# A two-layer gated trunk on one core: Silu in one ScalarE function, another order in the first output pair, the last merged chunk turned a slot later

## The chip, the cores and the metric

The kernel runs on one core of one Trainium2 chip. The metric is the device time of one execution in microseconds (us). All tensors are float32.

## What is computed

The reference is a trunk of two layers over a sequence of 256 positions with a model width of 2048:

```
for l in range(2):
    h = rms_norm(x, mix_norm[l])
    q, k, v, uv, gate_logits = split(h @ w_in[l])
    branch_a = sliding_window_attention(rope(rms_norm(q)), rope(rms_norm(k)), v, sinks[l]) @ w_attn_branch[l]
    branch_b = chunked_sgu(gelu(uv), ...) @ w_sgu_branch[l]
    gates = sigmoid(gate_logits)
    merged = gates[:, :2048] * branch_a + gates[:, 2048:] * branch_b
    x = x + merged @ w_out[l]
    h2 = rms_norm(x, ffn_norm[l])
    x = x + (silu(h2 @ w_gate[l]) * (h2 @ w_up[l])) @ w_down[l]
```

The hidden width of the last line is 5632, that is 11 chunks of 512 columns. The change touches the product with `w_out`, the norm behind it and the `silu` line.

## The kernel before, in words

**Entries.** Every product with a weight is cut into *entries*: 256 rows of a weight by a chunk of 512 columns. An entry is one DMA of 512 KB into a tile `raw` (line 202, on SyncE's queue), one ScalarE copy that rounds it to `whi` (L228), one VectorE subtraction that gives the rest `wlo` (L229), and the matmuls at L324 and L325. These take three terms: `whi` times the high part `uh` of the activations, `wlo` times `uh`, `whi` times the low part `ul`. A common entry has 12 matmuls of 128 x 512. Two chunks of columns that share their activations go as a *pair*: the first four 256 x 512 blocks of a pair are done by a seven-product scheme (entries P1 to P7, six matmuls each; some need a VectorE subtraction of weights at L213, and results are kept and moved at L346 to L352), and the rest by common entries, G for the first chunk and U for the second (lines 129 to 149). For the seven products, chunk 0 of the activations is needed whole (`uh`, `ul`) and as four sums of its quarters (`sh`, `sl`).

**Order.** The list `entries` (lines 172 to 186) fixes TensorE's order. The head of a pair (P1, P5, P2, P6, P7, P4) is woven into the last entries of the plan ahead of it. `Stream.next` (L233) loads seven entries ahead and splits four ahead. `whi` and `wlo` have four buffers each, so the split of an entry can only start when TensorE is done with the entry four before it. TensorE's instructions stand as they are written; for the other engines a scheduler sets the order of what is written.

**Slots.** All other work is put into slots by `after(n, fn)`: `fn` is written n slots later, and a slot is one common entry or two of six matmuls (lines 246 to 255, 359 to 363).

**Turning.** Activations are turned (transposed) for use as the stationary side, in `transposed` (L404). Mostly VectorE transposes blocks of 32 x 32 into a tile `box` (L393), and sixteen DMAs of 32 KB gather them into `tt` (L399), all on GpSimd's queue or, with `queue=None`, every second one on SyncE's. With `on_pe`, TensorE turns them into `pt` by eight small matmuls (L436). Then ScalarE makes `uh` (L418, L422, or `flat` at L463 and `uh` at L467 for chunk 0), and VectorE makes `ul` (L419, L427, L468). There is one `box`.

**Around the change.** The four chunks of `merged` are made by the four products `sgu` (line 944): VectorE adds the branches per half of the positions at L947 and L949 into the tile `gate`. Chunk 3, the last, is turned on TensorE (`on_pe`) three slots after its sums. The pair of chunks 0 and 1 of `w_out` follows ("first output pair"), then the pair of chunks 2 and 3 ("second output pair"), then the FFN's pairs of `w_gate` and `w_up`. When a chunk of the output is done, `residual` (L867) adds it into `xs` at L875, turns it two slots later for the FFN (`nxt.unit`), and squares it for the norm (L505). Chunk 0 goes through the steps of `WINO_NORM`, six numbers of slots counted from the turn: two scalings, the split, two groups of sums, the split of the sums. The norm's factor r (`rstd`) is applied only when products leave PSUM.

**The FFN's gate.** With g the gate product before r, `on_gate` (L965 to L968) takes th = tanh(r g / 2) on ScalarE (L967, scale `rhalf`), and (th + 1) g on VectorE (L968); `on_up` multiplies by the up product and by r r / 2 (`rr`, L972). It runs for 11 chunks in each of two layers, with two halves of the positions each.

Of the kernel before, what the change touches and what calls it, by code (L numbers as in the profile page):

```python
# [10 lines left out]
AF = mybir.ActivationFunctionType  # L11
# [17 lines left out]
NCH = D // CW  # L29
# [2 lines left out]
W_LOAD = 7  # L32
ROUNDS = ((0, 4), (4, 8), (8, 11))
WINO = 0
WINO_NORM = 7, 8, 10, 11, 12, 13
WINO_IN = 6, 7, 8, 12, 13, 14
WINO_FIRST = 6, 7, 8, 9, 10, 11
WINO_MIX = 6, 7, 9, 10, 11, 13
# [19 lines left out]
def hybrid_trunk(ctx: ExitStack, tc: tile.TileContext, x, mix_norm, w_in, q_norm, k_norm, sinks,  # L58
# [28 lines left out]
    def tiny(n, name, bufs=None):  # L87
        return small.tile([P, n], F32, tag=f"{name}{n}", name=nm(name), bufs=bufs)
# [32 lines left out]

        return Plan(key, [], [half(w, h, "X") for h in range(w.shape[0] // (2 * P))])

    def pair(key, wa, wb, by_unit=False):

        h1, h2 = 2 * WINO, 2 * WINO + 1
        l11, l12, l21, l22 = (load_of(w, h, t) for w, h, t in ((wa, h1, "k11"), (wb, h1, "k12"), (wa, h2, "k21"),  # L130
                                                              (wb, h2, "k22")))
        k11, k12, k21, k22 = l11[0], l12[0], l21[0], l22[0]
        rest = [h for h in range(wa.shape[0] // (2 * P)) if h // 2 != WINO]
        g, u = [half(wa, h, "G") for h in rest], [half(wb, h, "U") for h in rest]
        head = [dict(tag="P1", loads=[l11, l12], src=k11),
                dict(tag="P5", loads=[], sums=[(k11, k12, k11)], src=k11),
                dict(tag="P2", loads=[l21, l22], src=k21),
                dict(tag="P6", loads=[], sums=[(k11, k22, k11)], src=k11),
                dict(tag="P7", loads=[], sums=[(k12, k22, k12)], src=k12),
                dict(tag="P4", loads=[], sums=[(k21, k21, k11)], src=k21)]  # L140
        p3 = dict(tag="P3", loads=[], src=k22)
        body = g[:2] + [g[2], p3] + g[3:] + u
        g[1]["then"] = "open"
        if by_unit:
            body = g[:2] + [p3] + u[:2]
            g[0]["then"] = g[1].pop("then")
            for i in range(2, len(rest), 2):
                body += g[i:i + 2] + u[i:i + 2]
        return Plan(key, head, body)

    plans = []
    for l in range(DEPTH):
# [12 lines left out]
        c_ = cols_of(w_out[l], NCH)  # L165
        plans += [pair(("mix", l), c_[j], c_[j + 1]) for j in range(0, NCH, 2)]
        for r, (f0, f1) in enumerate(ROUNDS):
            for f in range(f0, f1):
                plans.append(pair(("ffn", l), w_gate[l, :, f * CW:(f + 1) * CW], w_up[l, :, f * CW:(f + 1) * CW], f == 0))
            c_ = cols_of(w_down[l, f0 * CW:f1 * CW, :], NCH)  # L170
            plans += [pair(("hid", l, r), c_[j], c_[j + 1], j == 0) for j in range(0, NCH, 2)]
# [155 lines left out]
    def step():  # L327
        e = entries[stream.at]
        p, tag = e["plan"], e["tag"]
        units = units_at[p.key]  # L330
        w = stream.next()
        if tag in "XGU":
            ps = banks(p, "b" if tag == "U" else "a")
            todo = [(ps[t], block(units, e["h"], t)) for t in range(NT)]
        else:
            sh, sl = units[WINO][2:]
            which, t, form = {"P1": ("a", 1, (0, 0)), "P2": ("a", 0, (1, 0)), "P6": ("a", 1, 1), "P7": ("a", 1, 2),
                              "P4": ("a", 1, (1, 1)), "P5": ("a", 0, 0), "P3": ("b", 0, 3)}[tag]
            todo = [(banks(p, which)[t], (sh[:, form], sl[:, form]) if isinstance(form, int)
                     else block(units, 2 * WINO + form[0], form[1]))]  # L340
        for ps, u in todo:
            add_product(p, ps, u, w, tag in ("P4", "P7"))
        a, b = p.acc.get("a"), p.acc.get("b")
        if tag == "P5":
            p.kept = slot([P, 2, CW], name="kept")
            nc.scalar.activation(p.kept[:, 1, :], a[0], AF.Copy)  # L346
            nc.scalar.activation(a[0], a[1], AF.Copy)
        elif tag in ("P6", "P7"):
            nc.vector.tensor_tensor(out=p.kept[:, int(tag == "P7"), :], in0=a[1], in1=p.kept[:, 1, :], op=ALU.add)  # L349
        if "then" in e:  # L350
            for t, ps in enumerate(banks(p, "b")):
                nc.scalar.activation(ps, p.kept[:, t, :], AF.Copy)  # L352
                p.opened.add(id(ps))
        p.left -= 1
        if e is getattr(p, "last_g", None):
            p.calls[0](a)
        if p.left == 0 and p.paired:
            p.calls[1](b)
        debt[0] += len(todo)
        if debt[0] >= 2:  # L360
            debt[0] -= 2
            if p.left or p.paired:
                tick()
# [130 lines left out]
    class Norm:  # L494
# [17 lines left out]
                       WINO_NORM)  # L512

        def finish(self):
            self.r, self.rh, self.rr = [], [], []
            for t in range(NT):
                v = tiny(1, f"var{t}", 2)
                nc.vector.tensor_reduce(out=v, in_=self.ss[t], axis=AX.X, op=ALU.add)
                nc.vector.tensor_scalar(out=v, in0=v, scalar1=1.0 / D, scalar2=EPS, op0=ALU.mult, op1=ALU.add)
                r_ = tiny(1, f"rstd{t}", 2)  # L520
                rsqrt(r_, v, 1)
                rh = tiny(1, f"rhalf{t}", 2)
                nc.vector.tensor_scalar(out=rh, in0=r_, scalar1=0.5, scalar2=None, op0=ALU.mult)
                rr = tiny(1, f"rr{t}", 2)
                nc.vector.tensor_tensor(out=rr, in0=r_, in1=rh, op=ALU.mult)
                self.r.append(r_)
                self.rh.append(rh)
                self.rr.append(rr)

    norm = Norm(first_cols)  # L530
    units_at["in", 0] = norm.units
# [335 lines left out]
    def residual(key, nxt=None, scale=1.0, store=False):  # L867

        def chunk(j, sums):
            for t in range(NT):  # L870
                n = 2 if store and j == NCH - 1 else 1
                w = CW // n
                for i in range(n):
                    sl = slice(j * CW + i * w, j * CW + (i + 1) * w)
                    nc.vector.scalar_tensor_tensor(out=xs[:, t, sl], in0=sums[t][:, i * w:(i + 1) * w], scalar=scale,  # L875
                                                   in1=xs[:, t, sl], op0=ALU.mult, op1=ALU.add)
                    if store:
                        eng = nc.sync if i == 0 else nc.scalar
                        eng.dma_start(out[0, t * P:(t + 1) * P, sl], xs[:, t, sl])
            if nxt is not None:  # L880
                last = j == NCH - 1 and not nxt.soon
                after(1 if last else 2, lambda: nxt.unit(j, j > 0 and nxt.soon, queue=None if last else nc.gpsimd,
                                                         late=-2 if last else 0))
                after(3, lambda: nxt.squares(j))
                if j == NCH - 1:
                    after(4, lambda: nxt.finish())
# [8 lines left out]
    for l in range(DEPTH):  # L895
# [43 lines left out]
        for j in range(NCH):  # L939
# [6 lines left out]
            for t in range(NT):  # L946
                nc.vector.scalar_tensor_tensor(out=gb[:, t, :], in0=gb[:, t, :], scalar=1.0, in1=ps[t],  # L947
                                               op0=ALU.add, op1=ALU.mult)
                nc.vector.tensor_tensor(out=ga[:, t, :], in0=ga[:, t, :], in1=gb[:, t, :], op=ALU.add)  # L949
            after(2 + (j == NCH - 1), lambda j=j, ga=ga: transposed(mT, j, ga, on_pe=j == NCH - 1,  # L950
                                                                   wino=WINO_MIX if j == WINO else None,
                                                                   late=3 if j == NCH - 2 else 0))
            tick()
# [7 lines left out]
        def hidden(hT, c):  # L961
            hid = slot([P, NT, CW], name="hid")

            def on_gate(g):
                for t in range(NT):  # L965
                    th = hid[:, t, :]
                    nc.scalar.activation(th, g[t], AF.Tanh, scale=norm.rh[t])  # L967
                    nc.vector.scalar_tensor_tensor(out=th, in0=th, scalar=1.0, in1=g[t], op0=ALU.add, op1=ALU.mult)  # L968

            def on_up(up):  # L970
                for t in range(NT):
                    nc.vector.scalar_tensor_tensor(out=hid[:, t, :], in0=up[t], scalar=norm.rr[t], in1=hid[:, t, :],  # L972
                                                   op0=ALU.mult, op1=ALU.mult)
                pe, soon = c == len(hT) - 1 == 2, c == 3
                after(3 if pe else 1 if soon else 2,
# [54 lines left out]
```

## Time and profile before

| | |
|---|---|
| median of 3 runs | 2469.17 us (2469.06 to 2469.82) |
| the profiled execution: its time / the span in its trace | 2468.67 us / 2467.0 us |
| TensorE (PE) busy, share of the span | 2452.7 us, 99% |
| VectorE (DVE) / ScalarE (ACT) / GpSimd (POOL) busy | 78% / 58% / 13% |
| granted TensorE clock over the span | 0.999 |
| DMA | 505.69 MB, mean 205 GB/s |

How to read it: a busy TensorE says that matmuls overlap in the records without a hole, not how fast they follow each other; a loss there shows as a larger step from one start to the next, or in the list of waits. SPq is SyncE's DMA queue. In a row of the timeline stand the start, the time taken, the engine, the line, the operation, the tiles, and in brackets how long the engine had been idle before and what ended that. Rows that follow each other with the same names are merged ("x2").

### The profile page before, as it was taken

The page shows a single profiled execution, that of the slowest core. Times are in us where ns is not written, and L with a number is a line of the kernel's source. Part 1 is how long each engine was busy: PE and PEld are TensorE (multiplying, and loading weights), DVE is VectorE, ACT ScalarE, POOL GpSimd, SP SyncE. Part 2 cuts the span into 40 slices and gives each one's busy share as a digit, 9 for nine tenths or more (in the row PEclk, how much of TensorE's full clock was granted, in tenths as well). Part 3 has the DMA queues.
Part 4 walks back from the last instruction along what each step waited for, and adds up shares of the span by engine and source line. Part 5 has one row for each costly group of instructions (what it writes and reads, how often), then busy time and mean ns, then how long its engine had stood idle before and what let it go on. Part 6 is the DMA issues. An engine that isn't in the chain of part 4 may idle for free.

```text
span 2467.0 us, 31322 instructions
## 1 busy us (share of the span) xinstructions
PE 2452.7 (99%) x11040; PEld 2027.6 (82%) x11040; DVE 1932.5 (78%) x2274; ACT 1431.0 (58%) x1793; POOL 309.3 (13%) x576
## 2 busy tenths in 40 slices
PE   9999999999999999999999999999999999999999
PEld 7888888888888888888887888888888888888887
DVE  6798676888877787778887986767888777877786
ACT  5567544565655565556655665455656555655564
POOL 3100002232110111001101000022311101110110
PEclk9999999999999999999999999999999999999999
DMA  9555667676666667576747446676767666666664
GB/s 293 199 187 162 214 197 220 184 235 205 216 210 202 216 193 234 180 225 190 225 153 265 154 154 225 205 213 182 236 198 233 200 216 195 219 207 203 215 195 146
DMA packets 279502, 505.69 MB, mean 205 GB/s; under 512 B 27760, under 2 KB 39120, under 8 KB 279344
## 3 DMA queue, kind: packets, MB, share of 16 engines
q1 hardware_dynamic: 261776, 485.83, 61.7%
q0 software_dynamic: 17248, 17.59, 2.7%
q8 instruction: 86, 1.41, 0.2%
q14 instruction: 72, 0.59, 0.1%
q10 hardware_dynamic: 320, 0.27, 0.0%
HBM read 475.27 MB, written 2.10 MB: 194 GB/s over the span
## 4 chain that ended last, share of the span: by engine, by line
PE 95%; DMA 2%; DVE 2%; SPq 1%; ACT 0%; issue 0%; POOL 0%; DVEq 0%; ACTq 0%
PE acc L324 61%; PE acc L325 31%; DMA raw<-in_w_in_dram 2%; DVE wlo L229 1%; PE po L780 1%; SPq L399 1%; PE psc L741 0%; PE ppt L770 0%; PE pt L436 0%; ACT whi L228 0%; PE psg L858 0%; POOL rq L296 0%; DVE box L393 0%; DVE ul L427 0%; DVE raw L213 0%
## 5 line engine op out<-in xcount | busy, mean ns | idle before, releaser
L229 DVE TENSOR_TENSOR wlo<-raw,whi 128x1024 fp32r<-128x1024 f32 (+1 forms) x1039 | 1261.8, 1220 | 478.8 <-ACT whi L228 465.7
L228 ACT ACTIVATE whi<-raw 128x1024 fp32r<-128x1024 f32 (+1 forms) x1038 | 1097.6, 1059 | 908.5 <-PE acc L325 709.9
L324 PE MATMUL acc<-whi,uh 128*128 128x512 f32 x3114 | 1216.6, 391 | 0.9 <-ACT uh L422 0.9
L324 PE MATMUL acc<-wlo,uh 128*128 128x512 f32 x3114 | 1213.3, 390 | 1.8 <-DVE wlo L229 1.8
L325 PE MATMUL acc<-whi,ul 128*128 128x512 f32 x3114 | 1212.8, 389 | 0.0
L324 PEld LDWEIGHTS acc<-wlo,uh 128*128 128x128 f32 x3114 | 585.2, 188 | 124.7 <-DVE wlo L229 4.2
L325 PEld LDWEIGHTS acc<-whi,ul 128*128 128x128 f32 x3114 | 585.0, 188 | 122.4 <-DVE ul L427 0.5
L324 PEld LDWEIGHTS acc<-whi,uh 128*128 128x128 f32 x3114 | 585.0, 188 | 121.7 <-ACT uh L422 1.1
L399 POOL DMA_DIRECT2D tt<-box x528 | 259.6, 499 | 1710.2 <-DMA raw<-in_w_up_dram 503.6
L213 DVE TENSOR_TENSOR raw<-raw,raw 128x1024 f32<-128x1024 f32 x188 | 229.4, 1220 | 1.3
L324 PE MATMUL acc<-whi,sh 128*128 128x512 f32 x376 | 147.2, 391 | 0.0
L324 PE MATMUL acc<-wlo,sh 128*128 128x512 f32 x376 | 146.9, 391 | 0.0
L325 PE MATMUL acc<-whi,sl 128*128 128x512 f32 x376 | 146.4, 389 | 0.0
L325 PEld LDWEIGHTS acc<-whi,sl 128*128 128x128 f32 x376 | 70.6, 188 | 14.8
L324 PEld LDWEIGHTS acc<-wlo,sh 128*128 128x128 f32 x376 | 70.6, 188 | 14.7 <-DVE kept L349 0.4
L324 PEld LDWEIGHTS acc<-whi,sh 128*128 128x128 f32 x376 | 70.6, 188 | 14.3
L349 DVE TENSOR_TENSOR kept<-acc,kept 128x512 f32<-128x512 f32 x94 | 64.3, 684 | 0.0
L352 ACT ACTIVATE acc<-kept 128x512 f32<-128x512 f32 x94 | 55.0, 586 | 11.0 <-DVE kept L349 10.9
L875 DVE SCALAR_TENSOR_TENSOR xs<-acc,xs 128x512 f32<-128x512 f32 (+1 forms) x66 | 41.4, 667 | 7.8 <-PE acc L325 7.8
L967 ACT ACTIVATE hid<-acc,rhalf 128x512 f32<-128x512 f32 x44 | 30.4, 690 | 20.7 <-PE acc L325 20.7
L419 DVE TENSOR_TENSOR ul<-tt,uh 128x512 fp32r<-128x512 f32 x52 | 34.0, 685 | 2.9 <-ACT uh L418 2.9
L968 DVE SCALAR_TENSOR_TENSOR hid<-hid,acc 128x512 f32<-128x512 f32 x44 | 29.6, 684 | 8.3 <-ACT hid L967 8.3
(137 smaller groups left out, 874.9 us busy)
## 6 DMA issues: line engine op xcount, KB each, us to landing
raw<-in_w_in_dram SPq DMA_DIRECT2D x239, 512.0 KB, 4.8
raw<-in_w_up_dram SPq DMA_DIRECT2D x176, 512.0 KB, 5.0
raw<-in_w_gate_dram SPq DMA_DIRECT2D x176, 512.0 KB, 4.3
raw<-in_w_down_dram SPq DMA_DIRECT2D x176, 512.0 KB, 5.0
raw<-in_w_out_dram SPq DMA_DIRECT2D x64, 512.0 KB, 5.1
tt<-box POOLq DMA_DIRECT2D x528, 32.0 KB, 4.4
raw<-in_w_attn_branch_dram SPq DMA_DIRECT2D x32, 512.0 KB, 5.5
raw<-in_w_sgu_branch_dram SPq DMA_DIRECT2D x32, 512.0 KB, 4.4
```

Of the source, the lines that this page charges most:

```text
L213: self.last = nc.vector.tensor_tensor(out=self.raws[d], in0=self.raws[x], in1=self.raws[y], op=ALU.subtract)
L228: self.high = nc.scalar.activation(hi[:, i, :], raw[:, i, :], AF.Copy)
L229: self.last = nc.vector.tensor_tensor(out=lo[:, i, :], in0=raw[:, i, :], in1=hi[:, i, :].bitcast(F32), op=ALU.subtract)
L324: nc.tensor.matmul(ps, a, part[:, kk, :], start=first and kk + n == 0, stop=False, skip_group_check=True)
L325: nc.tensor.matmul(ps, b, hi[:, kk, :], start=False, stop=kk == 1, skip_group_check=True)
L349: nc.vector.tensor_tensor(out=p.kept[:, int(tag == "P7"), :], in0=a[1], in1=p.kept[:, 1, :], op=ALU.add)
L352: nc.scalar.activation(ps, p.kept[:, t, :], AF.Copy)
L399: q.dma_start(dst[j * B:(j + 1) * B, i], box[i * B:(i + 1) * B, j])
L419: nc.vector.tensor_tensor(out=l, in0=s_, in1=h.bitcast(F32), op=ALU.subtract)
L875: nc.vector.scalar_tensor_tensor(out=xs[:, t, sl], in0=sums[t][:, i * w:(i + 1) * w], scalar=scale, in1=xs[:, t, sl], op0=ALU.mult, op1=AL ...
L967: nc.scalar.activation(th, g[t], AF.Tanh, scale=norm.rh[t])
L968: nc.vector.scalar_tensor_tensor(out=th, in0=th, scalar=1.0, in1=g[t], op0=ALU.add, op1=ALU.mult)
```

## The change

Four things are changed. First, `on_gate` is one ScalarE function per half, Silu with scale r, straight from the product; L968 is gone, `on_up` multiplies by r instead of `rr`, and `rr` is no longer made. Second, in the first output pair (`last_later`) the two entries U2 and U3 of the second chunk stand ahead of G6 and G7, the two of the first chunk that read the last merged chunk; the first chunk is therefore done two entries later. Third, the last merged chunk is turned four slots after its sums, not three. Fourth, since chunk 0 of the residual comes two slots later, the six steps of `WINO_NORM` count two less, and its gather goes half over SyncE's queue. The lookup of the sums in `step` is only made when an entry needs them.

```
-WINO_NORM = 7, 8, 10, 11, 12, 13
+WINO_NORM = 5, 6, 8, 9, 10, 11
...
         body = g[:2] + [g[2], p3] + g[3:] + u
         g[1]["then"] = "open"
+        if last_later:
+            body = g[:2] + [g[2], p3, g[3]] + u[:2] + g[4:] + u[2:]
...
-        plans += [pair(("mix", l), c_[j], c_[j + 1]) for j in range(0, NCH, 2)]
+        plans += [pair(("mix", l), c_[j], c_[j + 1], last_later=j == 0) for j in range(0, NCH, 2)]
...
-            sh, sl = units[WINO][2:]
...
-            todo = [(banks(p, which)[t], (sh[:, form], sl[:, form]) if isinstance(form, int)
+            todo = [(banks(p, which)[t], tuple(x[:, form] for x in units[WINO][2:]) if isinstance(form, int)
...
-                rr = tiny(1, f"rr{t}", 2)
-                nc.vector.tensor_tensor(out=rr, in0=r_, in1=rh, op=ALU.mult)
...
-                after(1 if last else 2, lambda: nxt.unit(j, j > 0 and nxt.soon, queue=None if last else nc.gpsimd,
+                after(1 if last else 2, lambda: nxt.unit(j, j > 0 and nxt.soon, queue=None if last or j == WINO and not nxt.soon else nc.gpsimd,
...
-            after(2 + (j == NCH - 1), lambda j=j, ga=ga: transposed(mT, j, ga, on_pe=j == NCH - 1,
+            after(2 + 2 * (j == NCH - 1), lambda j=j, ga=ga: transposed(mT, j, ga, on_pe=j == NCH - 1,
...
-                    th = hid[:, t, :]
-                    nc.scalar.activation(th, g[t], AF.Tanh, scale=norm.rh[t])
-                    nc.vector.scalar_tensor_tensor(out=th, in0=th, scalar=1.0, in1=g[t], op0=ALU.add, op1=ALU.mult)
+                    nc.scalar.activation(hid[:, t, :], g[t], AF.Silu, scale=norm.r[t])
...
-                    nc.vector.scalar_tensor_tensor(out=hid[:, t, :], in0=up[t], scalar=norm.rr[t], in1=hid[:, t, :],
+                    nc.vector.scalar_tensor_tensor(out=hid[:, t, :], in0=up[t], scalar=norm.r[t], in1=hid[:, t, :],
```

The changed kernel's lines stand two or so higher or lower than those of before, which is why the same operation has another number below.

On TensorE, layer 0, in the first output pair: the turn of the last merged chunk (`pt` from `gate`) before the change, behind the entry G2 (`whi_4126`) and ahead of G3 (`whi_4139`):

```order
L324 MATMUL acc_4021<-wlo_4127,uh_3757 128x512
L325 MATMUL acc_4021<-whi_4126,ul_3758 128x512
L436 MATMUL pt_4191<-ident,gate_2778 128x128 x4
L436 MATMUL pt_4198<-ident,gate_2778 128x128 x4
L324 MATMUL acc_4020<-whi_4139,uh_3757 128x512
L324 MATMUL acc_4020<-wlo_4140,uh_3757 128x512
```

The same place with the change, where `whi_4135` is now G3 and `whi_4157` is G4:

```order
L326 MATMUL acc_4017<-wlo_4136,uh_3753 128x512
L327 MATMUL acc_4017<-whi_4135,ul_3754 128x512
L437 MATMUL pt_4209<-ident,gate_2774 128x128 x4
L437 MATMUL pt_4216<-ident,gate_2774 128x128 x4
L326 MATMUL acc_4016<-whi_4157,uh_3853 128x512
L326 MATMUL acc_4016<-wlo_4158,uh_3853 128x512
```

The eight small matmuls have moved behind the 12 matmuls of G3; layer 1 reads alike.

On VectorE, layer 0, where the second output pair ends and the FFN's first pair begins, before the change; `wlo_4748` is the split of entry U5 of the second output pair, `wlo_4817` of its U6, `ul` from `tt` the low part of chunk 1 for the FFN, and `box` from `xs` the turn of chunk 2:

```order
L229 TENSOR_TENSOR wlo_4748<-raw_4675,whi_4747 128x1024
L229 TENSOR_TENSOR wlo_4785<-raw_4599,whi_4784 128x1024
L393 STREAM_TRANSPOSE box_4730<-xs 128x4x4x32 x2
L229 TENSOR_TENSOR wlo_4800<-raw_4677,whi_4799 128x1024
L213 TENSOR_TENSOR raw_4601<-raw_4679,raw_4601 128x1024
L427 SCALAR_TENSOR_TENSOR ul_4550<-tt_4551,vcols,uh_4549 128x128 x8
L229 TENSOR_TENSOR wlo_4817<-raw_4745,whi_4816 128x1024
```

The same place with the change; U5 is `wlo_4744` and U6 is `wlo_4813`:

```order
L231 TENSOR_TENSOR wlo_4744<-raw_4671,whi_4743 128x1024
L394 STREAM_TRANSPOSE box_4726<-xs 128x4x4x32 x2
L428 SCALAR_TENSOR_TENSOR ul_4546<-tt_4547,vcols,uh_4545 128x128 x8
L231 TENSOR_TENSOR wlo_4781<-raw_4593,whi_4780 128x1024
L231 TENSOR_TENSOR wlo_4796<-raw_4673,whi_4795 128x1024
L215 TENSOR_TENSOR raw_4595<-raw_4675,raw_4595 128x1024
L231 TENSOR_TENSOR wlo_4813<-raw_4741,whi_4812 128x1024
```

The turn of chunk 2 and the low part of chunk 1 now stand ahead of two weight splits instead of between and behind them; on ScalarE the high part of chunk 1 (L422) has moved in the same way, from behind the splits of P6 and P2 to ahead of them.

On ScalarE, layer 0, the FFN's first gate before the change (`hid` is the gate's tile):

```order
L228 ACTIVATE whi_5196<-raw_5146 128x1024
L967 ACTIVATE hid_4924<-acc_4737,rhalf_964_5003 128x512
L967 ACTIVATE hid_4924<-acc_4738,rhalf_968_5012 128x512
L228 ACTIVATE whi_5218<-raw_5018 128x1024
L228 ACTIVATE whi_5232<-raw_5177 128x1024
```

The same place with the change:

```order
L230 ACTIVATE whi_5188<-raw_5138 128x1024
L964 ACT_TABLE_LOAD
L964 ACTIVATE hid_4920<-acc_4733,rstd_961_4997 128x512
L964 ACTIVATE hid_4920<-acc_4734,rstd_964_5004 128x512
L230 ACTIVATE whi_5208<-raw_5010 128x1024
L230 ACTIVATE whi_5222<-raw_5169 128x1024
```

A load of ScalarE's function table has come in ahead of the first Silu; there is another in layer 1 at the same place, and one ahead of layer 1's first Exp of the attention scores, three that were not there. On SyncE's queue eight gather DMAs of chunk 0 stand, in each layer, between the weight loads of entries G5 and G6 of the second output pair.

More of the change, by code (lines that the diff above doesn't have):

```diff
@@ L122, in single, with pair @@
         return Plan(key, [], [half(w, h, "X") for h in range(w.shape[0] // (2 * P))])
-    def pair(key, wa, wb, by_unit=False):
+    def pair(key, wa, wb, by_unit=False, last_later=False):
         h1, h2 = 2 * WINO, 2 * WINO + 1
@@ L514, in finish @@
         def finish(self):
-            self.r, self.rh, self.rr = [], [], []
+            self.r, self.rh = [], []
             for t in range(NT):
@@ L523, in finish @@
                 nc.vector.tensor_scalar(out=rh, in0=r_, scalar1=0.5, scalar2=None, op0=ALU.mult)
-                rr = tiny(1, f"rr{t}", 2)
-                nc.vector.tensor_tensor(out=rr, in0=r_, in1=rh, op=ALU.mult)
                 self.r.append(r_)
                 self.rh.append(rh)
-                self.rr.append(rr)
     norm = Norm(first_cols)
```

## The prediction, made blind

> **What bounds the kernel now.** I read the page first, for the chain of work that ended last, and then the list of what TensorE (PE) waited for.
>
> ```profile
> span 2467.0 us, 31322 instructions
> ...
> PE 95%; DMA 2%; DVE 2%; SPq 1%; ACT 0%; issue 0%; POOL 0%; DVEq 0%; ACTq 0%
> ```
>
> TensorE makes up 95% of the chain. A change that gives it no less to multiply can only win where it stands. The list of its waits has seven rows, of which these are the first three:
>
> ```profile
> PE pt L436 <- DVE gate L949: 2.9, 2, 1.4
> PE ppt L770 <- DVE wsT L641: 2.3, 1, 2.3
> PE acc L324 <- DVE wlo L229: 1.8, 5, 0.6
> ```
>
> The first row is the turn of the last merged chunk (L436), which waits for the sum at L949 once in each layer, 2.9 us in two waits of about 1.4. The change touches this row. The second and third belong to the start and to the attention, and there the order of the engines stays as it was but for a table load (below). In the FFN, where most of the changed instructions are, TensorE waits for nothing. So the gain that is there to be had is about 3 us, and the rest of the work is to see what the change could spoil.
>
> **The turn, one slot later.** TensorE in layer 0, then in layer 1:
>
> ```profile
> 463.69 0.27 PE L436 MATMUL pt<-ident,gate 128*128 128x128 f32 x1
> 465.41 0.98 PE L436 MATMUL pt<-ident,gate 128*128 128x128 f32 x7 [1.45 <-DVE gate L949]
> 466.15 0.48 PE L324 MATMUL acc<-whi,uh 128*128 128x512 f32 x1
> ```
>
> ```profile
> 1690.73 0.27 PE L436 MATMUL pt<-ident,gate 128*128 128x128 f32 x1
> 1692.44 0.66 PE L436 MATMUL pt<-ident,gate 128*128 128x128 f32 x4 [1.45 <-DVE gate L949]
> ```
>
> From the second turn to the matmul behind the last pass 466.15 - 465.41 = 0.74, or 0.11 for each of seven. From the first turn to the second pass 1.72 in layer 0 and 1.71 in layer 1. So 1.61 and 1.60 are lost, together **3.2 us**. The list's 2.9 is the lower bound: it counts only the hole behind the modelled end of the first turn. VectorE (DVE) at that place in layer 0:
>
> ```profile
> 460.06 1.22 DVE L229 TENSOR_TENSOR wlo<-raw,whi 128x1024 fp32r<-128x1024 f32 x1
> ...
> 462.39 2.36 DVE L229 TENSOR_TENSOR wlo<-raw,whi 128x1024 fp32r<-128x1024 f32 x2
> 464.66 0.69 DVE L949 TENSOR_TENSOR gate<-gate,gate 128x512 f32<-128x512 f32 x1
> ```
>
> The sum of the second half of the positions ends at 464.66 + 0.69 = 465.35, behind two weight splits. With the change TensorE does G3 first. The pace of its matmuls can be read from the two Tanh rows further down (578.07 and 579.43): each was let go by the last of six matmuls, and they are 1.36 apart, 0.227 for a matmul. G3's twelve take 2.72, so the turn comes up at 463.69 + 2.72 = 466.41, 1.06 after the sum. It no longer waits.
>
> What is late instead? G3 is wanted 2.5 earlier than it was, at 463.69; its split is the row at 460.06, over at 461.28. G4 follows the turn at about 467.3; its split is the first of the two at 462.39, over at 463.6. Both are there. Then the turned chunk itself:
>
> ```profile
> 466.62 1.29 DVE L419 TENSOR_TENSOR ul<-pt,uh 128x512 fp32r<-128x512 f32 x2
> ```
>
> Its low part was ready at 467.9, 1.8 after the turn's end at 466.15. With the change one weight split stands ahead of it, some 1.2 more, so 3.0 after the turn. The first entry that reads it is G6, and G4, P3, G5, U2 and U3 stand ahead of that: 54 matmuls, 12.2 us. There are 9 us to spare; without U2 and U3 there would still be 3.8. Moving these two entries is the same matmuls in another order and costs TensorE nothing.
>
> **Chunk 0 of the next norm, two slots later.** The first chunk of the pair ends two entries or 5.4 us later, while the steps of `WINO_NORM` stay where they were. So the gather has 5.4 less to be done in, and goes half over SyncE:
>
> ```profile
> 488.78 5.00 POOL L399 DMA_DIRECT2D tt<-box  x10 [45.63 <-PE acc L325]
> ```
>
> ```profile
> 554.64 5.28 SPq L399 DMA_DIRECT2D tt<-box  x8
> ```
>
> ```profile
> 509.65 1.69 ACT L463 ACTIVATE flat<-tt,vcols 128x256 f32<-128x256 f32 x4
> ```
>
> ```profile
> tt<-box POOLq DMA_DIRECT2D x528, 32.0 KB, 4.4
> ```
>
> It starts at 488.78 + 5.4 = 494.2. GpSimd's eight take 4.0 to issue (ten took 5.00) and land 4.4 later, at 502.6. SyncE's eight hold its queue for 5.3, by the row for another chunk, until 499.5. ScalarE reads the tile at 509.65. With 7 us of cover this costs nothing. Behind SyncE's eight stand weight loads:
>
> ```profile
> 500.22 0.37 SPq L202 DMA_DIRECT2D raw<-in_w_out_dram  x1
> ```
>
> ```profile
> 511.37 1.06 ACT L228 ACTIVATE whi<-raw 128x1024 fp32r<-128x1024 f32 x1
> ```
>
> ```profile
> raw<-in_w_out_dram SPq DMA_DIRECT2D x64, 512.0 KB, 5.1
> ```
>
> The first of them, for G6 of the second output pair, was issued at 500.22, lands 5.1 later and is read at 511.37. That leaves 6.0, and the queue is free again by 499.5. Nothing, then; the loads for the FFN's head, which now come behind it, are read later still.
>
> **Silu.** It takes 44 VectorE products away and puts one function in the place of another:
>
> ```profile
> L967 ACT ACTIVATE hid<-acc,rhalf 128x512 f32<-128x512 f32 x44 | 30.4, 690 | 20.7 <-PE acc L325 20.7
> ...
> L968 DVE SCALAR_TENSOR_TENSOR hid<-hid,acc 128x512 f32<-128x512 f32 x44 | 29.6, 684 | 8.3 <-ACT hid L967 8.3
> ```
>
> ```profile
> L272 ACT ACT_TABLE_LOAD x1 | 1.3, 1283 | 1.3 <-PEq L1008 1.3
> ```
>
> VectorE loses 44 x 0.684 = 30 us of work. TensorE waits for nothing in the FFN, so that is worth 0. Silu isn't in the trace. From below it can't beat a plain copy of half a weight split's size, 1.06 / 2 = 0.53 by the row at 511.37; from above I allow two passes, 2 x 0.690 = 1.38. I take Tanh's 0.690, the row for the same shape, source and kind of scale. Three table loads are new, 1.28 each by the one row there is. The first Silu's place and what follows it:
>
> ```profile
> 578.07 0.69 ACT L967 ACTIVATE hid<-acc,rhalf 128x512 f32<-128x512 f32 x1 [0.30 <-PE acc L325]
> 579.43 0.69 ACT L967 ACTIVATE hid<-acc,rhalf 128x512 f32<-128x512 f32 x1 [0.67 <-PE acc L325]
> 580.01 2.00 ACT L228 ACTIVATE whi<-raw 128x1024 fp32r<-128x1024 f32 x2
> ```
>
> ```profile
> 583.67 3.65 DVE L229 TENSOR_TENSOR wlo<-raw,whi 128x1024 fp32r<-128x1024 f32 x3
> ```
>
> ```profile
> 586.26 0.39 PE L324 MATMUL acc<-wlo,uh 128*128 128x512 f32 x1
> ```
>
> The load starts at 578.07, where Tanh did, and is over at 579.35. The halves of Silu follow 0.58 apart (579.43 to 580.01), so the weight copies start at 580.51 and not at 580.01, 0.5 late. The first of them, for P7, is over by 581.6. VectorE then has P7's split, a weight subtraction and U7's split, each 1.22 (a third of 3.65): over at 585.3, where before it was 583.67 + 1.22 = 584.9. TensorE reads U7's low part at 586.26. About 1.0 of cover is left and nothing is lost. With a Silu of 1.38 the copies would be late by 1.9 and U7's split over at 586.7, a loss of 0.4 in each layer, 0.9 in all; the later pairs have no table load and lose nothing. The load ahead of layer 1's first Exp waits for nothing, and falls into a hole of 3.03 on ScalarE:
>
> ```profile
> 1338.27 0.40 ACT L758 ACTIVATE pr<-pr,negm 128x128 f32<-128x128 f32 x1 [3.03 <-DVE negm L751]
> ```
>
> **The sum.** The profiled execution took 2468.67, of which 2467.0 are its span. Less 3.2 that is 2465.5. The median of the runs shown, 2469.17, stands 0.5 above this execution, so I predict **2466.0**, 0.13% less than before.
>
> **The rivals.** *First, slower: ScalarE asks for chunk 1 too early.* This is the thinnest place I found, where the FFN's first pair begins:
>
> ```profile
> 527.69 1.06 ACT L228 ACTIVATE whi<-raw 128x1024 fp32r<-128x1024 f32 x1 [0.30 <-PE acc L325]
> ```
>
> ```profile
> 518.70 2.58 POOL L399 DMA_DIRECT2D tt<-box  x5 [0.65 <-DMA tt<-box]
> ```
>
> ```profile
> 531.50 1.23 DVE L229 TENSOR_TENSOR wlo<-raw,whi 128x1024 fp32r<-128x1024 f32 x1 [0.58 <-ACT whi L228]
> ...
> 538.21 2.35 DVE L229 TENSOR_TENSOR wlo<-raw,whi 128x1024 fp32r<-128x1024 f32 x2
> ```
>
> ```profile
> 539.91 0.39 PE L324 MATMUL acc<-wlo,uh 128*128 128x512 f32 x1
> ```
>
> ```profile
> ACT qT L725 <- DMA tt<-box: 18.9, 4, 5.5
> ```
>
> U6's split (the first at 538.21) was over at 539.4, 0.5 before TensorE read it. In the new order the same VectorE work fills the hole of 0.58, which is good for some 0.6 more. But ScalarE now wants the gathered chunk 1 at 527.69 + 1.06 = 528.7, ahead of two splits. Its last DMA was issued by 521.3 and lands 4.4 later at 525.7, or up to 1.2 later if its turn slips by one split: 1.8 of cover. A gather that lands later first eats some 1.2 in which VectorE turns chunk 2, then U6's 1.1; past a wait of about 2.3 TensorE pays one for one, in both layers. ScalarE has waited for a gather as long as 5.5 elsewhere. Such a wait would cost 2 x (5.5 - 2.3) = 6.4, less the 3.2 gained: **2472.4**. Past 6.4 of wait the kernel would be slower by over 0.2%. Against it speaks that the same read found its data there before, though two splits later.
>
> *Second, ScalarE stands longer at a change of table than the load itself.* U7's cover of 1.0 is the point from which it decides; with a stop 1.3 longer, as long again as the load, 2 x 0.3 = 0.6 is given back: **2466.6**. [...]
>
> *Third, the turn still waits,* as if the change didn't do what it says: the sum would have to slip along with the turn. The splits ahead of it hang on entries that TensorE has done by then, so I see no reason for it. Then **2469.2**, as before.
>
> *Fourth, more goes than that.* If the wait of 2.3 in layer 1's attention went too, because loads land otherwise there: 2466.0 - 2.3 = **2463.7**.
>
> **How the numbers follow.** Forecast 0.67, first rival 0.08, second 0.13, third 0.06, fourth 0.06. A measurement of this kernel can tell about 0.2%, 4.9 us, from no change, so faster means below 2464.2 and slower above 2474.1. Faster is the fourth, 0.06. Slower is the part of the first with longer waits, 0.04. All else, 0.90, is within. The forecast's own range is 2465.3 to 2466.6, from 2.9 in place of 3.2 and from the spread of the three runs (2469.06 to 2469.82). The range goes down to 2464.8, which takes a little of the fourth, and up to 2468.0: the dear end of Silu (0.9), or a stall of 1.0 in each layer at the thin place.
>
> **What would show it.** Right: the row of L949 is gone from TensorE's waits, VectorE is busy for 30 us less, no new wait of TensorE stands in the FFN, Silu takes 0.69, and the table loads lie in ScalarE's holes. Wrong: a wait for `wlo` or `uh` where the FFN's first pair begins (first rival), one at U7 of that pair (second), Silu rows well above 0.69, or the turn's wait still there.

## The result, and the profile after

The changed kernel takes **2467.05 us** (median of 21 runs, 2464.09 to 2469.26) where the kernel before, beside it on the chip, takes 2470.18 (21 runs, 2467.79 to 2472.93). The ratio is 0.9984 with a 95% interval of 0.9978 to 0.999: 3.1 us less, by the interval between 2.5 and 5.4. Forecast were 3.2 less and no difference beyond 0.2%, and so it came.

The page of the changed kernel, an execution of 2464.09 us, the fastest of its 21:

```profile
span 2462.4 us, 31291 instructions
...
PE 2451.1 (100%) x11040; PEld 2026.7 (82%) x11040; DVE 1903.8 (77%) x2222; ACT 1435.0 (58%) x1796; POOL 299.6 (12%) x560
```

VectorE has lost its 44 products, and nothing in the time comes of that (e2 below). What does come is seen in TensorE's waits (what waited, for what, us in total, times, longest), of which the longest is now:

```profile
PE ppt L768 <- DVE wsT L639: 2.4, 1, 2.4
```

The row that led the list before, `pt` waiting for `gate`, is gone, and no new one stands in the output pairs or the FFN. The turn itself in TensorE's timeline, layer 0 and layer 1:

```profile
465.35 0.39 PE L327 MATMUL acc<-whi,ul 128*128 128x512 f32 x1
465.58 1.03 PE L437 MATMUL pt<-ident,gate 128*128 128x128 f32 x8
466.37 0.48 PE L326 MATMUL acc<-whi,uh 128*128 128x512 f32 x1
...
1690.88 1.03 PE L437 MATMUL pt<-ident,gate 128*128 128x128 f32 x8
1691.67 0.48 PE L326 MATMUL acc<-whi,uh 128*128 128x512 f32 x1
```

All eight small matmuls now run as one group (x8, no bracket), 0.79 from the turn's first matmul to the next entry, in both layers. Before, layer 0 took from 463.69 to 466.15, 2.46. So 1.67 is gained there. When the matmuls of the entries are lined up one by one in the two traces, the step at the turn is 1.67 in layer 0 and 1.67 in layer 1. VectorE at that place:

```profile
463.84 0.68 DVE L947 TENSOR_TENSOR gate<-gate,gate 128x512 f32<-128x512 f32 x1
464.44 1.22 DVE L231 TENSOR_TENSOR wlo<-raw,whi 128x1024 fp32r<-128x1024 f32 x1
...
468.01 1.28 DVE L420 TENSOR_TENSOR ul<-pt,uh 128x512 fp32r<-128x512 f32 x2
```

The sum ends at 464.52, still behind weight splits; it is TensorE that comes later.

**The two profiled spans differ by 4.6, which is too much.** Some of it is the start. TensorE in the kernel before:

```profile
10.72 0.63 PE L324 MATMUL acc<-whi,uh 128*128 128x512 f32 x1
...
13.96 0.47 PE L324 MATMUL acc<-whi,uh 128*128 128x512 f32 x1
```

And in the changed kernel, at the same place in the program:

```profile
9.92 0.39 PE L326 MATMUL acc<-whi,uh 128*128 128x512 f32 x1
...
12.10 0.48 PE L326 MATMUL acc<-whi,uh 128*128 128x512 f32 x1
```

The same matmul takes 0.63 in one execution and 0.39 in the other; the granted clock is 0.50 from 9.60 to 13.01 in the first. No edit touches this place. The second entry starts 1.86 earlier in the execution of after, and the starts of later entries (lined up one by one in the two traces) show 0.86 of that still there at 127 us. The medians, not the two profiles, give the size of the effect.

### The profile page after: what moved, and what is told of

Read it like the earlier page. It is cut to its first block, busy times and chain, and to the rows that moved or that the text cites. A ratio compares the mean times of both kernels' runs of the same rounds, so it can differ in the third digit from the quotient of the medians.

```text
span 2462.4 us, 31291 instructions
## 1 busy us (share of the span) xinstructions
PE 2451.1 (100%) x11040; PEld 2026.7 (82%) x11040; DVE 1903.8 (77%) x2222; ACT 1435.0 (58%) x1796; POOL 299.6 (12%) x560
## 4 chain that ended last, share of the span: by engine, by line
PE 96%; DMA 2%; DVE 1%; SPq 1%; issue 0%; ACT 0%; DVEq 0%; ACTq 0%
PE acc L326 62%; PE acc L327 31%; DMA raw<-in_w_in_dram 2%; PE po L778 1%; PE psc L739 1%; PE ppt L768 1%; DVE wlo L231 0%; SPq L400 0%; ACT whi L230 0%; PE psg L856 0%; PE pt L437 0%; DVE ul L428 0%; DVE sq L684 0%; DVE q L678 0%; DVE raw L215 0%
## 5 line engine op out<-in xcount | busy, mean ns | idle before, releaser
L400 POOL DMA_DIRECT2D tt<-box x512 | 250.9, 497 | 1714.0 <-DVE box L394 619.1
L964 ACT ACTIVATE hid<-acc,rstd 128x512 f32<-128x512 f32 x44 | 30.1, 690 | 19.1 <-PE acc L327 19.0
L347 ACT ACTIVATE kept<-acc 128x512 f32<-128x512 f32 x47 | 28.0, 597 | 12.9 <-PE acc L327 12.9
```

Source lines behind the costliest of these rows:

```text
L400: q.dma_start(dst[j * B:(j + 1) * B, i], box[i * B:(i + 1) * B, j])
L964: nc.scalar.activation(hid[:, t, :], g[t], AF.Silu, scale=norm.r[t])
```

## The experiments

Three questions: which of the edits made the gain, whether the edits that did nothing were cover for something, and what bounds the kernel next. Ratios are to the kernel before, run beside each, with 95% intervals.

**e1, the turn alone.** On the kernel before:

```
-            after(2 + (j == NCH - 1), lambda j=j, ga=ga: transposed(mT, j, ga, on_pe=j == NCH - 1,
+            after(2 + 2 * (j == NCH - 1), lambda j=j, ga=ga: transposed(mT, j, ga, on_pe=j == NCH - 1,
```

> The kernel before with one edit alone: the last merged chunk is turned four slots after its sums, not three. Theory (the whole gain is the turn's wait): both waits of about 1.6 us go, 3.2 us less than before (ratio 0.9987), the row of the gate sum is gone from TensorE's waits, and no new wait stands at G6, since G4, P3 and G5 (30 matmuls, 6.8 us) still cover the 3.0 us in which the turned chunk is made. Rival A (VectorE's lighter load has a share): less than 3.2 us here. Rival B (the two entries moved ahead are needed): the wait comes back at G6 in another name, and the time is as before.

Measured: 2466.17, ratio 0.9984 (0.9975 to 0.9993). This one number gives what the whole change gives. TensorE's longest wait is now another:

```profile
PE ppt L770 <- DVE wsT L641: 2.5, 1, 2.5
```

The row of `gate` is gone here too, without the moved entries U2 and U3.

**e2, Silu alone.** On the kernel before:

```
-                    th = hid[:, t, :]
-                    nc.scalar.activation(th, g[t], AF.Tanh, scale=norm.rh[t])
-                    nc.vector.scalar_tensor_tensor(out=th, in0=th, scalar=1.0, in1=g[t], op0=ALU.add, op1=ALU.mult)
+                    nc.scalar.activation(hid[:, t, :], g[t], AF.Silu, scale=norm.r[t])
...
-                    nc.vector.scalar_tensor_tensor(out=hid[:, t, :], in0=up[t], scalar=norm.rr[t], in1=hid[:, t, :],
+                    nc.vector.scalar_tensor_tensor(out=hid[:, t, :], in0=up[t], scalar=norm.r[t], in1=hid[:, t, :],
```

> The kernel before with Silu alone in place of tanh and the product. Theory: VectorE is busy for 30 us less, Silu takes 0.69 us, three table loads of 1.28 us lie in holes, both waits of the turn (2.9 us in the list) stay, and the time is that of before (ratio 1.000). Rival A: 1 us or more less, from waits for weight splits that a lighter VectorE shortens. Rival C (a change of table is dear): 0.5 to 1 us more, at the FFN's first pair of each layer.

Measured: 2471.06, ratio 1.0006 (0.9997 to 1.0015), with the turn's wait as it was:

```profile
PE pt L436 <- DVE gate L949: 2.9, 2, 1.4
```

**e3, the order of the output pair, the gather's queue and the norm's steps alone,** with the turn in its old slot. The diff is that of the change without its turn and its Silu:

```
-WINO_NORM = 7, 8, 10, 11, 12, 13
+WINO_NORM = 5, 6, 8, 9, 10, 11
...
+        if last_later:
+            body = g[:2] + [g[2], p3, g[3]] + u[:2] + g[4:] + u[2:]
```

> The kernel before with the reorder alone: U2 and U3 ahead of G6 and G7 in the first output pair, the six steps of chunk 0 counted two less, its gather half on SyncE's queue; the turn stays three slots after the sums. Theory: the same matmuls in another order, both waits of the turn stay (2.9 us in the list), the time is that of before (ratio 1.000). Rival B (the reorder makes the gain): 3.2 us less. Rival D (the gather on SyncE's queue holds weight loads): up to 5 us more in each layer, waits for weight splits in the second output pair.

Measured: 2469.31, ratio 1.0000 (0.9991 to 1.0009), and the same wait:

```profile
PE pt L437 <- DVE gate L950: 2.9, 2, 1.4
```

The three parts thus give 0.9984, 1.0006 and 1.0000, and together 0.9984. The gain is the turn's. But a part that gives nothing alone may still be cover, so the turn was next moved further.

**e6 and e7, the turn two slots later still,** without the moved entries (e6, on the kernel before) and with them (e7, on the changed kernel):

```
-            after(2 + (j == NCH - 1), lambda j=j, ga=ga: transposed(mT, j, ga, on_pe=j == NCH - 1,
+            after(2 + 4 * (j == NCH - 1), lambda j=j, ga=ga: transposed(mT, j, ga, on_pe=j == NCH - 1,
```

> The kernel before with the turn six slots after the sums, that is directly ahead of G6, which reads the turned chunk; the order of the entries as before. Theory: the wait of the turn goes (3.2 us), but nothing covers the 1.8 to 3.0 us in which the chunk is made, and G6 waits 1 to 3 us in each layer for its high or low part: between 1 us less and 3 us more than before. Rival (TensorE needs only the first half of the chunk, which is made in 0.6 us each of copy and subtraction): under 1 us of wait in each layer, 1.2 to 3.2 us less than before.

> The changed kernel with the turn six slots after the sums; U2 and U3 (24 matmuls, 5.4 us) stand between the turn and G6. Theory: the cover of 5.4 us is more than the 3.0 us in which the chunk is made, no wait in either place, and the time is that of the changed kernel; against the run without cover this shows what the two moved entries are good for. Rival: the chunk's steps are held up on ScalarE and VectorE by the splits of the next entries by more than 5.4 us, and G6 waits as without cover.

Measured: e6 2470.51, ratio 1.0003 (0.9993 to 1.0012); e7 2466.13, ratio 0.9989 (0.998 to 0.9998). In e6 TensorE has two new waits in each layer, 1.5 us in all for `uh` and 1.3 for `ul`. The timeline shows how they follow from the turn, in layer 0, TensorE first, then ScalarE and VectorE:

```profile
474.83 1.03 PE L436 MATMUL pt<-ident,gate 128*128 128x128 f32 x8
476.63 0.50 PE L324 MATMUL acc<-whi,uh 128*128 128x512 f32 x1 [0.76 <-ACT uh L418]
...
478.00 0.50 PE L325 MATMUL acc<-whi,ul 128*128 128x512 f32 x1 [0.64 <-DVE ul L419]
...
475.03 1.06 ACT L228 ACTIVATE whi<-raw 128x1024 fp32r<-128x1024 f32 x1 [1.66 <-DMA raw<-in_w_out_dram]
476.00 1.07 ACT L418 ACTIVATE uh<-pt 128x512 fp32r<-128x512 f32 x2
...
476.12 1.23 DVE L229 TENSOR_TENSOR wlo<-raw,whi 128x1024 fp32r<-128x1024 f32 x1 [1.49 <-ACT whi L228]
477.26 1.28 DVE L419 TENSOR_TENSOR ul<-pt,uh 128x512 fp32r<-128x512 f32 x2
```

The turn is followed at once by the entry that reads the turned chunk. Its high part waits behind one weight split on ScalarE, its low part behind one on VectorE. What was gained at one end is paid back at the other. With U2 and U3 between (e7) these two waits are not in TensorE's list. So the reorder is real cover, good for two more slots than the change uses; at four slots e1 shows that it isn't needed.

**e4, chunk 0 gathered by GpSimd alone.** On the changed kernel:

```
-                after(1 if last else 2, lambda: nxt.unit(j, j > 0 and nxt.soon, queue=None if last or j == WINO and not nxt.soon else nc.gpsimd,
+                after(1 if last else 2, lambda: nxt.unit(j, j > 0 and nxt.soon, queue=None if last else nc.gpsimd,
```

> The changed kernel with the gather of chunk 0 wholly on GpSimd's queue again. Theory: sixteen issues take 8 us from about 494 and land 4.4 us later, at 506.6, still ahead of ScalarE's read at about 507 to 509 (the changed kernel runs 2.5 us earlier there); the cover shrinks to 0 to 3 us, and the time is that of the changed kernel within 0.5 us. Rival (the half on SyncE's queue is needed): ScalarE waits for the gather, and with it the splits; 1 to 3 us more per layer.

Measured: 2468.14, ratio 0.9994 (0.9985 to 1.0004), about 1.1 us above the change's median, and 1.4 and 2.0 above e5 and e7, which ran on the same chip. The intervals of these ratios overlap, so it is the trace that has to carry the reading. My expectation of no more than 0.5 missed. In the changed kernel the halves go like this, GpSimd, then SyncE's queue with the weight load behind it, then ScalarE's read:

```profile
493.65 3.91 POOL L400 DMA_DIRECT2D tt<-box  x8 [51.35 <-DVE box L394]
...
493.39 4.97 SPq L400 DMA_DIRECT2D tt<-box  x8
498.45 0.53 SPq L204 DMA_DIRECT2D raw<-in_w_out_dram  x1
...
507.16 1.70 ACT L464 ACTIVATE flat<-tt,vcols 128x256 f32<-128x256 f32 x4
```

In e4, GpSimd, ScalarE, VectorE and, where entry U6 of the second output pair reads its split, TensorE:

```profile
495.71 5.39 POOL L400 DMA_DIRECT2D tt<-box  x11 [51.33 <-DVE box L394]
...
504.12 1.56 POOL L400 DMA_DIRECT2D tt<-box  x3 [1.46 <-DMA tt<-box]
...
514.57 1.69 ACT L464 ACTIVATE flat<-tt,vcols 128x256 f32<-128x256 f32 x4
...
538.34 2.35 DVE L231 TENSOR_TENSOR wlo<-raw,whi 128x1024 fp32r<-128x1024 f32 x2
...
539.25 0.39 PE L326 MATMUL acc<-whi,uh 128*128 128x512 f32 x1
539.61 0.50 PE L326 MATMUL acc<-wlo,uh 128*128 128x512 f32 x1
```

GpSimd no longer issues at its own pace of 0.49: from the thirteenth on it stops for its earlier DMAs, 1.46 at the longest, and ends at 505.7; the last gather has landed at 510.8. ScalarE's read stands 7.4 later than in the changed kernel, where this whole trace is 2.1 later (entry against entry). The late gather alone does not make it so late: the read starts 3.8 after the last landing. In ScalarE's order two more weight splits, at 510.93 and 513.61, now stand ahead of it, and these two entries, 2.7 each, are the other 5.3. The order is the scheduler's, which was given the gather on one queue; ScalarE waits for no DMA there, so the rival had the place right and the wait wrong. VectorE's share of the norm comes later with the read, U6's split is over at 538.34 + 1.22 = 539.56, and TensorE steps by 0.36 and not 0.23. From 537.42 to 540.14 in the changed kernel's time, this trace loses 0.6 in layer 0, and as much at the same place in layer 1. By this trace the moved order needs the second queue: the edit is no gain but repairs what the reorder costs. The place is the one named as the thinnest in the first rival.

**e5, two tables in every FFN pair.** On the changed kernel, a one-column Exp (of the gate times zero, into a scratch tile that nothing reads) ahead of each pair's first Silu:

```
+                nc.scalar.activation(tiny(1, "sw", 2), g[0][:, :1], AF.Exp, scale=0.0)
```

> The changed kernel with one more instruction ahead of each pair's first Silu: an Exp of one column of the gate product, times 0, into a tile that nothing reads. Exp and Silu are in different tables, so there are two loads in every one of the 22 pairs, 44 in all. Theory (a change of table costs the 1.28 us of its load and nothing more): ScalarE is 2.8 us late once in each pair, the cover of the ordinary pairs (U7's and its neighbours' splits, 2.9 us) takes it, and at most 1 us is lost at the first pair of each layer: 0 to 3 us more than the changed kernel. Rival C (a drain of about the load's length comes with each): 5.4 us late in each pair, 2.5 us of TensorE waits in each, 50 us more.

Measured: 2466.75, ratio 0.9987 (0.9977 to 0.9996). Two of ScalarE's groups:

```profile
L965 ACT ACT_TABLE_LOAD x22 | 28.2, 1283 | 0.1
...
L963 ACT ACT_TABLE_LOAD x20 | 25.7, 1283 | 0.4
```

There are 42 loads in the FFN, two in nearly every pair, and the ratio stays within 0.0003 of the change's. In all 42 the function starts within 0.02 us of the load's end, so no stop beyond the load's 1.28 is in the rows. The loads cost what their rows say, and ScalarE has holes for them.

**e8, the next wait in the list.** `wsT` is made by eight small matmuls (`pw`) and a copy on VectorE. On the changed kernel:

```
-        after(40, pl.spatial)
+        after(38, pl.spatial)
```

> The changed kernel with one more edit: the eight turns of the spatial weights (L640 of before) are written 38 slots after the layer's start, not 40. TensorE's longest remaining wait, 2.4 us in layer 1, is for VectorE's copies of them, which stand behind two weight splits whose copies on ScalarE are late. Theory (a wait of TensorE counts in full, whatever else is busy): the copies now stand ahead of these splits, the wait goes, 2.4 us less than the changed kernel, 5.6 us less than before (ratio 0.9977). Rival: the late splits themselves are next, and less than 1 us is won; or the copies in layer 0 come to stand ahead of something that TensorE waits for, and nothing is won.

Measured: 2463.33, ratio 0.9973 (0.9963 to 0.9983). In the changed kernel, layer 1, TensorE and VectorE:

```profile
1345.61 1.03 PE L638 MATMUL pw<-ident,wsraw 128*128 128x128 f32 x8
...
1349.65 0.65 PE L768 MATMUL ppt<-ident,pr 128*128 128x128 f32 x4 [2.36 <-DVE wsT L639]
...
1346.44 2.56 DVE L231 TENSOR_TENSOR wlo<-raw,whi 128x1024 fp32r<-128x1024 f32 x2 [5.69 <-ACT whi L230]
1348.91 1.28 DVE L639 COPY wsT<-pw 128x512 f32<-128x512 f32 x2
```

And in e8:

```profile
1340.65 1.03 PE L638 MATMUL pw<-ident,wsraw 128*128 128x128 f32 x8
...
1347.73 0.66 PE L768 MATMUL ppt<-ident,pr 128*128 128x128 f32 x4
...
1377.90 0.50 PE L326 MATMUL acc<-wlo,sh 128*128 128x512 f32 x1 [0.91 <-DVE kept L350]
...
1341.28 1.29 DVE L639 COPY wsT<-pw 128x512 f32<-128x512 f32 x2
```

It is the turn's mechanism again: a small VectorE step behind two weight splits, with TensorE waiting for it (`ppt` and `pw` take their buffers from the same pair in `ps_tr`). Two slots earlier the copy falls into VectorE's hole. Entry against entry e8 gains 2.4 on the changed kernel's profile at this wait, and gives 1.5 of it back within the next 50 us, most of that in the new wait of 0.9.

**e9, e10 and e11: is e8's lead real, and are Silu and the reorder needed for it?** On one chip: the kernel before with e1's and e8's numbers alone (e9), e8's kernel again (e10), and the changed kernel again (e11).

> The kernel before with two numbers changed: the turn one slot later (as in the change) and the turn of the spatial weights at slot 38 in place of 40; no Silu, no reorder. Theory (the two waits are all there is to be had, Silu and the reorder add nothing): the gate row and the wsT row are both gone from TensorE's waits, and the time equals that of the changed kernel with slot 38, within 1 us. Rival (the reorder or Silu is needed for the second gain): 1 us or more slower than that kernel.

> The changed kernel with the turn of the spatial weights at slot 38, a second time, beside the changed kernel itself on one chip. Theory (its profile showed 0.8 to 1.1 us kept of the wsT wait, and the rest of its lead was the luck of the start): 0.8 to 1.5 us faster than the changed kernel. Rival (the earlier turn is worth more than the landmarks show): 2.5 us or more faster, as the medians of two different jobs said.

> The changed kernel itself, as the measure for the other two. Expected: 0.9984 of the kernel before, within its interval of 0.9978 to 0.999, so about 2466 to 2467 us; its start may differ from the first profile by up to 3 us.

Measured: e9 2463.49, ratio 0.9972 (0.996 to 0.9983); e10 2463.10, ratio 0.9971 (0.9959 to 0.9982); e11 2467.02, ratio 0.9984 (0.9974 to 0.9993). Two numbers in the kernel before do as much as the whole change with slot 38. And e10 is 3.9 faster than e11, where its profile is 2.0 shorter (2461.7 and 2463.7): my expectation of 0.8 to 1.5 fell, and the rival of 2.5 or more stands. At the wait for `wsT`, e10's trace gains 1.5 on e11's (3.0 less 1.5 that comes back).

**e12, a third profile of the changed kernel,** to see where its slower executions lose their time.

> The changed kernel, for a third profile. Theory (the wait for the turned spatial weights is longer in the slower runs, which is what the slot 38 kernels are rid of): if this run's span is 2465 or more, its wait of TensorE for wsT is 4 us or more, or other waits stand in layer 1's attention. Rival (the slower runs lose their time elsewhere): wsT as before, 2.4 to 3.0, and the time lost shows at another place.

Measured: 2466.70, span 2465.0. TensorE behind the wait for `wsT`:

```profile
1350.74 0.70 PE L768 MATMUL ppt<-ident,pr 128*128 128x128 f32 x4 [3.02 <-DVE wsT L639]
...
1351.67 0.63 PE L326 MATMUL acc<-wlo,uh 128*128 128x512 f32 x1
...
1354.65 0.40 PE L327 MATMUL acc<-whi,ul 128*128 128x512 f32 x1
```

The wait itself is no longer than e11's 3.0. But the matmuls behind it step by 0.43 and not 0.23, from 1351.67 to 1354.65: seven steps, 2.98 where 1.59 is the pace, so 1.4 lost, more by 0.2 with the two around them. Two stretches of 3.41 us each (from and to, length, busy time and instructions of five engines with TensorE first, granted clock, DMA share, GB/s) in e12, and then in e7, which has the longest such wait of all profiles (3.15, from 1348.02 to 1351.16):

```profile
1347.82:1351.23 3.41, 0.49 (x5) 0.49 (x5) 3.29 (x5) 3.11 (x4) 0.00 (x0) 1.00 1.04 390
1351.23:1354.64 3.41, 3.41 (x10) 2.65 (x9) 3.41 (x6) 1.63 (x3) 0.00 (x0) 0.50 0.81 294
```

```profile
1346.36:1349.77 3.41, 1.66 (x17) 1.29 (x15) 1.71 (x2) 2.63 (x4) 0.00 (x0) 1.00 1.05 401
1349.77:1353.18 3.41, 2.02 (x11) 1.76 (x12) 3.41 (x6) 2.90 (x6) 0.00 (x0) 1.00 1.05 384
```

In e12 the granted clock is 0.50 for one stretch of 3.41 us; in e7, behind a longer wait, it stays at 1.00. Neither theory had it (the rival had only the wait's length right): the wait has a second price, paid in some executions. Of the eleven profiles with this wait, e3, e4, e5 and e12 show slow matmuls behind it; of the three without it (e8, e9, e10) none does.

The traces also show which executions pay. In every one of the fourteen, the moments at which the granted clock changes lie whole multiples of 3.413 us apart (in the kernel before 9.60, 13.01 and, 719 steps of 3.4133 on, 2467.20), so in each trace they stand on a fixed grid of windows. The stretches above are windows of that grid. In e12, 2.93 of the wait's 3.02 fall into one window, and the next has half the clock; in e7 an edge at 1349.77 cuts the wait into 1.75 and 1.39. All eleven follow this: at least 2.0 of the wait in one window where the slow matmuls are (e5 2.02, e4 2.25, e3 2.58, e12 2.93), at most 1.75 where they are not. No run moved the grid on purpose.

## Why the prediction was right

*What bounds the kernel.* TensorE's own work, and beyond it only its waits, not the other engines' loads: 30 us less on VectorE is worth nothing (e2, 1.0006).

*The turn.* Predicted 1.61 and 1.60; measured 1.67 in each layer, and e1 with nothing else has the whole gain. The turn was to come up 1.06 after the sum. It comes at 465.58, and the sum ends at 464.52: 1.06. The chunk's low part was to be ready 3.0 after the turn; it is, at 469.29, 2.9 after 466.37.

*The moved entries.* Predicted: no cost, and still some slack without them. e1 and e3 bear out both; e6 finds the end of the slack.

*The gather.* Predicted 7 us between the last landing and the read. Measured: the sixteen land 2.4 to 3.8 after their issues, the last at 500.2, and the read is at 507.16, so 7.0. Both stand 2.4 to 2.5 earlier than in the prediction's numbers. SyncE is free at 498.4, and its next load goes out at 498.45. Nothing is lost. What I didn't work out is what the half on SyncE is worth: by e4's trace 0.6 in each layer.

*Silu and its tables.* ScalarE's group in the changed kernel, and the first Silu of layer 0 with what follows:

```profile
L964 ACT ACTIVATE hid<-acc,rstd 128x512 f32<-128x512 f32 x44 | 30.1, 690 | 19.1 <-PE acc L327 19.0
```

```profile
575.51 1.28 ACT L964 ACT_TABLE_LOAD   x1 [0.34 <-PE acc L327]
576.81 1.27 ACT L964 ACTIVATE hid<-acc,rstd 128x512 f32<-128x512 f32 x2
...
581.33 3.65 DVE L231 TENSOR_TENSOR wlo<-raw,whi 128x1024 fp32r<-128x1024 f32 x3
...
583.66 0.39 PE L326 MATMUL acc<-wlo,uh 128*128 128x512 f32 x1
```

Silu takes 0.690, the value taken from Tanh. U7's split is the first of the three, over at 582.55, and read at 583.66: 1.1 of cover, predicted 1.0.

*First rival.* False: ScalarE's `uh` of chunk 1 waits for no gather, and U6's split, over at 536.25, has 1.2 before its reader where it had 0.5:

```profile
526.16 1.69 ACT L423 ACTIVATE uh<-tt,vcols 128x256 fp32r<-128x256 f32 x4
...
535.03 1.22 DVE L231 TENSOR_TENSOR wlo<-raw,whi 128x1024 fp32r<-128x1024 f32 x1
...
537.42 0.39 PE L326 MATMUL acc<-wlo,uh 128*128 128x512 f32 x1
```

*Second rival.* False: the load ends at 575.51 + 1.28 = 576.79 and Silu starts at 576.81. No run shows the stop of 1.3 that this rival was added up from: the rows show 0.02 here, and with 42 loads (e5) nothing adds up either. *Third:* false, the row is gone. *Fourth:* not by this change, which leaves `wsT` at 2.4; but e8 and e9 show that the time was there.

*What I had too small* is the spread. The three runs shown spanned 0.8 us, and I took the forecast's own width from them; 21 runs of the kernel before span 5.1, and their median is 1.0 higher. The difference came out within 0.1 and the time itself 1.05 above the forecast. That is outside the forecast's own 2465.3 to 2466.6 and inside the wider range, but not for the reasons that the range was widened for: Silu was not dear, and nothing stalled at the thin place. The kernel before, whose three runs the sum starts from, is itself slower over 21 runs. By the time alone the second rival, at 2466.6, would be the nearer; it is the rows that decide against it.

## What to carry to other kernels

Before taking work off an engine, look whether anyone waits for it: 30 us of VectorE were worth nothing, and a slot number was worth 3.1. A small step that TensorE turns and another engine finishes is to be placed where that engine has a hole, with entries between the turn and its reader; of e6, e7 and e8 each shows one end of that. An edit that measures as nothing alone may be cover or repair for another (the entries U2 and U3, the gather's half on SyncE), so take it away in the company that it was made for.

## What the runs showed of the hardware

- **A wait of TensorE can cost more than its length.** Behind waits for `wsT` of 2.3 (e4) to 3.0 (e12) the granted clock is 0.50 for one window of 3.41 us, TensorE's matmuls step by 0.43 and not 0.23 for up to 3.0 us, and up to 1.6 is lost; in seven other profiles, with waits of 2.3 to 3.1, nothing of this is seen. Which executions have it follows where the edges of the window fall: with 2.0 us or more of the wait in one window it came, with 1.75 or less it did not. The window ahead of e5's slow stretch was not idle as a whole: TensorE was busy for 1.39 of its 3.41 us. Nor is 2.0 a general limit: at the start of e9 two holes of 0.79 and 0.76 in one window were followed by the same slow pace, matmuls of 0.63 that step by 0.43. A slow stretch also stands at the start of the profile of the kernel before (the matmul of 0.63 above, at a granted clock of 0.50 from 9.60 to 13.01).
- **What this makes of e10's 3.9** is settled in part. The record gives the mean granted clock of each execution, to three digits. e10's four executions at 1.000 have a median of 2462.90 and e11's three at 1.000 one of 2465.39, so about 2.5 of the 3.9 stands where both run at the full clock, on few executions. The rest comes with the executions at a lower clock, eight of e11's eleven and two of e10's six, and how much of it lies behind this wait is not settled.
- **GpSimd stops for its earlier gathers.** Eight go out at 0.49 each. Of sixteen, a later one waits, and not always the same: before the change the eleventh of chunk 0 (1.24), in e4 the thirteenth and fourteenth (0.42 and 1.46), in the changed kernel the ninth and eleventh of chunk 1 (0.65 and 1.42). What sets the number is open.
- **A change of ScalarE's table cost 1.28 and no more,** 42 times over (e5).
